# Second layer's output projection regrouped, its final quarter computed block by block with the norm's rows in PSUM; the first layer's conv taps and weight splits divided anew between the engines

## The chip, the cores and the metric

One core of one Trainium2 chip. The metric is the device time of one execution in microseconds (us): 1711.2 us, the median of 3 runs (1710.54 to 1713.39). Engines are called as in the profile: PE (matrix multiply), PEld (its weight loads), DVE (vector), ACT (scalar activation), POOL (general), SP (issues the DMAs).

## What is computed

A decoder block of two layers on 1024 tokens of 1024 channels, in float32.

```
layer 1:  a, g, z = split(x @ w_in + b_in)
          u = a * sigmoid(g);  u = causal depthwise conv(u), 31 taps, + b_dw
          u = silu(layer_norm_over_channels(u)) * silu(z)
          x1 = layer_norm(ALPHA * x + u @ w_out + b_out)
K, V    = x1 @ kv_w                       (three groups of 16 heads of 64)
layer 2:  q, z = split(x1 @ w_in)
          per head: 3 dilated windows of attention, merged by their softmax denominators -> o
          out = layer_norm(ALPHA * x1 + (o * silu(z)) @ w_out + b_out)
```

## The kernel before

Every product is made of three passes of a rounded type: each operand is split into a high part (a rounded copy) and a low part (the rest), and PE computes high x high, low x high and high x low into one PSUM bank. A weight of 128x1024 (512 KB) is loaded by SP (`wraw`), copied to `whi` (line 234 on ACT, 236 on POOL) and subtracted to `wlo` (line 243, on DVE if its running number is in `DVE_LO`, otherwise on POOL). `whi`, `wlo` and `wraw` have two buffers each.

**The order of the instructions** is made by a list scheduler (class `Order`): each step has an engine, a cost in us, a priority, the steps that it follows and the buffers that it takes and frees; a simulation with these costs picks, for each engine, the ready step with the lowest priority. The result is the order of each engine's queue; the costs are nowhere else in the program.

**Layer 1.** PE makes the projections `pa`, `pg` (8 channel blocks) and `pz`, in two halves of 512 tokens. The conv of each channel block and half has 31 taps: tap 0 is an ACT activation (line 400), taps 1 to n-1 are products on ACT (`cvt`, line 410) added on POOL (line 414), and taps n to 30 are fused multiply-adds on DVE (line 426) into a PSUM bank. n is `N_POOL`, 12 for the second halves of channels 4 to 7 and 10 for the other 12 convs. For those 12 ("merged") the two sums run side by side and one DVE add joins them (line 438); for the four others DVE starts from POOL's sum. The statistics of the channel norm follow (lines 451 to 505), then norm, silu and gate (lines 517 to 527), the split into `uh` and `ul` (532, 537), the output projection `po` (line 638) and the post-norm, whose result is transposed (`pt`, line 730) for layer 2.

**Layer 2** works by pairs of heads, eight of them; the matmuls of the next pair's projections (`pk`, `pq`, `pzb`, `pv`) lie between the small matmuls of the pair before. `finish` closes a pair: ACT widens the reciprocal denominators (`rx`), PE spreads them over the head's rows (`rb`, line 1302: four 128x128 products with the identity for each token half), DVE scales (line 1307), POOL multiplies by the gate (`on`, line 1312), ACT and DVE split. The joins of the two heads run on POOL (`op`, line 1275). Pairs 0 to 6 go through DRAM (`o_d`), the last pair directly into `uhb`/`ulb`.

**The out-projection of layer 2** has four quarters: token half h (outs[0], outs[1]) by column half ch. A quarter is 16 steps of 6 matmuls: four weights kp (channel blocks 2kp and 2kp+1) by four token blocks j, each j with its own PSUM bank. kp = 3 needs the last pair. Before, the last pair's attention was filled with kp 0 to 2 of quarters (0,0) and (0,1); then came kp 3 of (0,1) and (0,0), and then the two quarters of outs[1] whole, the last with its last two weights j by j. `evac` adds a bank to the residual `r` on DVE (lines 654 and 656; `r` was loaded from `x_d` and given the bias on POOL, line 610) and takes its statistics (line 663). `norm` then makes mean and 1/sd (672 to 683), centers on ACT (695), multiplies by the gain row (699) and adds the bias row (703), on DVE or POOL as `PATHS` says, and stores (707).

Of the kernel before, what the change touches and what calls it, by code (L numbers as in the profile page):

```python
# [28 lines left out]
N_POOL = dict.fromkeys(("d4", "d5", "d6", "d7"), 12)  # L29
# [4 lines left out]
DVE_LO = {0, 2, 3, 8, 9, 11, 12, 14, 15, 17, 19, 20, 23, 24, 25, 26, 27, 31, 33, 34, 35, 38, 39, 41, 42, 44, 45, 46, 90, 92, 93, 94, 98, 100, 101, 102, 103, 104, 105, 106, 108, 110, 111, 112, 113, 114, 115, 117, 118, 119, 124, 125, 126, 130, 131, 133, 134, 136}  # L34
PATHS = {(0, 1): 'dp', (1, 1): 'dd', (2, 1): 'pd', (3, 1): 'pd', (0, 0): 'pd', (2, 0): 'pd', (3, 0): 'dd'}
# [3 lines left out]
RELEASE = 0.25  # L39
ENGINES = ("pe", "act", "dve", "pool", "dma", "none")  # L40
# [9 lines left out]
class Step:  # L50
    def __init__(self, eng, cost, fn, prio, table, take):
        self.eng, self.cost, self.fn, self.prio, self.table, self.take = eng, cost, fn, prio, table, take
        self.waits, self.then, self.users, self.frees = 0, [], 0, []


class Order:
# [5 lines left out]
    def add(self, eng, cost, fn, prio, after=(), take=None, frees=(), table=None):  # L62
        step = Step(eng, cost, fn, prio, table, take)
# [12 lines left out]
    def run(self):  # L76
# [8 lines left out]
        while True:  # L85
# [28 lines left out]
            while events and events[0][0] <= now:  # L114
                _, _, _, other, step = heapq.heappop(events)
                for o in step.frees if other is None else ():
                    o.users -= 1
                    if not o.users:
                        live[o.take] -= 1
                for o in step.then:  # L120
                    if o.eng == other:
                        o.waits -= 1
                        if not o.waits:
                            heapq.heappush(heaps[other], (o.key, o))
# [6 lines left out]
def block_kernel(ctx: ExitStack, tc: tile.TileContext, x, xT, a_w_in, a_vec, a_w_out, rows,  # L131
# [74 lines left out]
    class Weight:  # L206


        def __init__(self, src, shape, pieces=1, hi_eng="act", spare=False):
# [4 lines left out]
            self.steps, self.spare = [], spare  # L214
# [3 lines left out]
        def piece(self, n, src, shape, i, pieces, hi_eng, hi_cost, lo_eng, lo_cost):  # L218
# [3 lines left out]
            @on("dma", 1.46 / pieces, (1, n) if pieces == 1 else (1, 0.5, 2 * i + 0.5, n), take=None if i else "raw")  # L222
            def fetch():
                if i == 0:
                    self.raw = wpool.tile([P] + shape, F32, name="wraw", tag="raw")
# [3 lines left out]
            @on(hi_eng, hi_cost, (0.5, n), [fetch], take=None if i else "b4" if self.spare else "whi")  # L229
# [8 lines left out]
            @on(lo_eng, lo_cost, (0.5, n), [hi], take=None if i else "b4" if self.spare else "wlo", frees=[self.first] if last else [])  # L238
# [7 lines left out]
        def part(self, name, shape):  # L246
            if self.spare:
                return b4(name, F32R).rearrange("p (k n) -> p k n", n=shape[1])
# [6 lines left out]
        def slots(self):  # L255
            return self.steps[0]
# [14 lines left out]
    def project(name, w, src, h, prio):  # L271
# [3 lines left out]
        def part(k):  # L275
            @on("pe", 0.68, prio + (k,), ([b.last] if k else []) + w.ready(k, KT) + src.steps[h][k],
# [166 lines left out]
    def mean_of(h, y, last):  # L443
# [3 lines left out]
        @on("pe", 0.86, (0, 0), [last, cst_in] + ([b.last] if b.first else h * [var[0].first]), take=None if b.first else "av")  # L447
# [62 lines left out]
    def apply(c, h, idx):  # L510
# [23 lines left out]
        @on("dve", 0.86, (0.5, c), [hi], take="hp", frees=[y.first])  # L534
# [49 lines left out]
    class Out:  # L584


        def __init__(self, h, row, src, prio, by_class=False):
# [4 lines left out]
            self.lazy = src is UA and h == 0  # L592
# [21 lines left out]
        def product(self, ch, kps, weight_of, banks, jk=False, end=False):  # L614
# [3 lines left out]
            if jk:  # L618
                cut = len(kps) - 2
                todo = todo[:4 * cut] + [(kp, j) for j in range(4) for kp in kps[cut:]]  # L620
            n = step_no("unit")
            for i, (kp, j) in enumerate(todo):
                self.part(ch, kp, j, ws[kp], banks[j], kp == kps[0], kp == kps[-1], n, i, end)

        def part(self, ch, kp, j, w, b, start, stop, n, i, end):
# [3 lines left out]
            @on("pe", 1.38, self.prio + (n, i), w.ready() + [s for k in ks for s in src[k, h].steps] +  # L629
                ([] if start else [b.last]), take=b.tag if start else None,  # L630
# [35 lines left out]
        def norm(self, j, dst_d, turned=None, paths={}):  # L666
# [18 lines left out]
            for ch in range(2):  # L685
                self.finish(j, ch, shift, dst_d, turned, paths.get((j, ch), "dp"))
# [226 lines left out]
    def scores23(a, g, o, gate):  # L913
# [24 lines left out]
        for i in range(2):  # L938
            bias = bias_of(a, g, i)
            part(i, 0.5, 0.83, [(slice(r * P, (r + 1) * P), slice(2 * r * P, (2 * r + 1) * P),  # L940
# [8 lines left out]
    def swap(made, prio):  # L949
# [4 lines left out]
        @on("pe", 0.25, prio, [made], take="cv")  # L954
# [90 lines left out]
    def vals(srcs, by_block, gate, n, end=False):  # L1045
# [26 lines left out]
        def part(t, kh, i):  # L1072
# [17 lines left out]
            @on("pe", 1.45, n + (i,), ws[kh].ready() + ready + ([b.last] if b.last else []),  # L1090
# [56 lines left out]
    def turn(a, blocks, after, frees):  # L1147
# [4 lines left out]
        @on("pe", 0.085 * n, (2.8, a.p, 4), after + a.flip, take="cv", frees=frees)  # L1152
# [136 lines left out]
    def finish(a, n):  # L1289
# [8 lines left out]
        @on("pe", 0.88, (2.8, a.p, 5), [widen] + a.turned[1], take="cv", frees=[widen])  # L1298
# [46 lines left out]
    for p in range(PAIRS):  # L1345
# [3 lines left out]
        a.sz, a.sz_step, a.op, a.op_slot, a.finished, a.stored = {}, {}, {}, {}, [], []  # L1349
# [31 lines left out]
    for h in range(2):  # L1381
        def fetch_u(h=h):
# [12 lines left out]
            for k in range(KT):  # L1395
                UB[k, h] = Box()
                UB[k, h].steps, UB[k, h].slots = list(got), []
# [12 lines left out]
    def weight_out(ch, kp, spare=False):  # L1410
# [102 lines left out]
```

## Time and profile before

| | |
|---|---|
| median of 3 runs | 1711.2 us |
| the profiled execution | 1710.37 us |
| its span, first to last instruction | 1708.6 us |
| PE / DVE / ACT / POOL busy, share of the span | 96% / 63% / 52% / 49% |
| mean granted clock of PE | 0.983 |
| layer 1 / layer 2 up to the last scores / last pair and out-projection | to about 436 us / to about 1563 us / to the end |

The page gives shares over the whole span, and the stages have different limits, so it is read by stretches. A line of the timeline has the start, the duration in us, the engine, the source line, the operation with its output and inputs, the number of instructions merged into the line, and in brackets the idle time before and what ended it. Durations of instructions in a row overlap, since each includes its latency: how often one can start is read from the starts.

### The profile page before, as it was taken

What the parts mean: (1) busy time and instruction counts of PE and PEld (TensorE: products, weight loads), DVE (VectorE), ACT (ScalarE), POOL (GpSimd) and SP (SyncE); (2) the same over time, 40 slices, a digit from 0 to 9 for tenths busy, and PEclk for the clock granted to TensorE, in tenths of its full rate; (3) what the DMA queues carried; (4) which work ended last, traced back from release to release, by engine and by line L of the source; (5) the groups of instructions that cost most, each with busy time, mean ns of one, the idle gap of its engine ahead of it and who ended that gap; (6) DMA issues with size and microseconds to landing.
All of it is one profiled execution on the core that took longest, in us unless ns stands there. A gap on an engine that the chain in (4) does not pass through costs nothing.

```text
span 1708.6 us, 25230 instructions
## 1 busy us (share of the span) xinstructions
PE 1637.9 (96%) x9396; PEld 1419.1 (83%) x9396; DVE 1074.4 (63%) x2293; ACT 887.9 (52%) x1986; POOL 834.1 (49%) x490
## 2 busy tenths in 40 slices
PE   8999968999899999999999999999999999999966
PEld 6888856767789988988988998898898899889855
DVE  7999999978664554554365365546536554653475
ACT  7666636265228525725743663664284275339432
POOL 5999957348333444444344435432432242233563
PEclk9999989999899999999999999999999999999988
DMA  5111111544211111101101101210120111135532
GB/s 190 50 50 41 59 37 50 174 140 155 74 38 38 38 38 62 37 29 65 45 26 48 64 26 38 66 47 25 38 75 26 38 62 38 38 103 186 193 99 86
DMA packets 43803, 116.67 MB, mean 68 GB/s; under 512 B 4512, under 2 KB 5792, under 8 KB 43680
## 3 DMA queue, kind: packets, MB, share of 16 engines
q1 hardware_dynamic: 43680, 115.06, 20.1%
q8 instruction: 74, 1.21, 0.3%
q14 instruction: 49, 0.40, 0.1%
HBM read 97.21 MB, written 17.83 MB: 67 GB/s over the span
## 4 chain that ended last, share of the span: by engine, by line
PE 69%; DVE 2%; ACT 1%; POOL 1%; DMA 1%; issue 0%; DVEq 0%; SPq 0%; POOLq 0%; ACTq 0%
PE pq L282 15%; PE pk L282 15%; PE pv L1099 15%; PE po L638 5%; PE pzb L282 5%; PE ptp L1156 4%; PE ps L866 3%; PE ps L867 3%; PE av L1175 2%; PE av L1172 2%; PE rb L1302 1%; DMA ulb<-o_d 1%; DVE x1b L1066 1%; POOL r L610 0%; DVE r L699 0%
## 5 line engine op out<-in xcount | busy, mean ns | idle before, releaser
L236 POOL TENSOR_SCALAR whi<-wraw 128x1024 fp32r<-128x1024 f32 x80 | 223.4, 2792 | 509.5 <-PE pv L1099 149.3
L243 POOL TENSOR_TENSOR wlo<-wraw,whi 128x1024 fp32r<-128x1024 f32 (+1 forms) x82 | 191.2, 2332 | 114.0 <-ACT whi L234 109.9
L414 POOL TENSOR_TENSOR y<-y,cvt 128x512 f32<-128x512 f32 x152 | 205.8, 1381 | 23.4 <-ACT cvt L410 18.6
L426 DVE SCALAR_TENSOR_TENSOR cva<-u,av,cva 128x512 f32<-128x512 f32 x308 | 209.0, 744 | 0.5
L822 DVE TENSOR_TENSOR kl<-pk,kd 64x512 fp32r<-64x512 f32 x192 | 132.2, 689 | 106.3 <-ACT kd L818 56.8
L1166 DVE TENSOR_TENSOR pl<-ptp,ph 128x384 fp32r<-128x384 f32 (+1 forms) x192 | 108.5, 587 | 105.1 <-ACT ph L1161 98.8
L870 DVE CUSTOM_DVE_ANT_0 s<-ps,bias 128x256 f32<-128x256 f32 (+1 forms) x384 | 122.6, 371 | 53.6 <-PE ps L867 53.3
L282 PE MATMUL pk<-x1h,whi 128*128 128x512 f32 x384 | 154.0, 401 | 0.0
L282 PE MATMUL pq<-x1h,whi 128*128 128x512 f32 x384 | 153.8, 401 | 0.0
L282 PE MATMUL pk<-x1h,wlo 128*128 128x512 f32 x384 | 150.6, 392 | 1.6 <-DVE wlo L243 1.6
L282 PE MATMUL pq<-x1h,wlo 128*128 128x512 f32 x384 | 150.7, 392 | 0.0
L282 PE MATMUL pq<-x1l,whi 128*128 128x512 f32 x384 | 150.5, 392 | 0.0
L282 PE MATMUL pk<-x1l,whi 128*128 128x512 f32 x384 | 150.2, 391 | 0.0
L852 ACT ACTIVATE qs<-pq 64x512 fp32r<-64x512 f32 x96 | 56.9, 593 | 174.3 <-PE pq L282 173.6
L1099 PE MATMUL pv<-whi,x1h 128*128 128x256 f32 x512 | 147.1, 287 | 0.0
L1099 PE MATMUL pv<-wlo,x1h 128*128 128x256 f32 x512 | 144.9, 283 | 0.0
L1099 PE MATMUL pv<-whi,x1l 128*128 128x256 f32 x512 | 144.9, 283 | 0.0
L410 ACT ACTIVATE cvt<-u,av 128x512 f32<-128x512 f32 x152 | 106.2, 719 | 53.9 <-POOL y L414 52.2
L818 ACT ACTIVATE kd<-pk 64x512 fp32r<-64x512 f32 x96 | 56.8, 592 | 141.7 <-PE pk L282 140.8
L1161 ACT ACTIVATE ph<-ptp 128x384 fp32r<-128x384 f32 (+1 forms) x192 | 93.0, 513 | 61.7 <-PE ptp L1156 47.2
L243 DVE TENSOR_TENSOR wlo<-wraw,whi 128x1024 fp32r<-128x1024 f32 (+1 forms) x60 | 98.9, 1649 | 32.2 <-POOL whi L236 16.9
L857 DVE TENSOR_TENSOR qs<-pq,qs 64x512 fp32r<-64x512 f32 x96 | 66.1, 688 | 77.4 <-ACT qs L852 75.1
(163 smaller groups left out, 4532.5 us busy)
## 6 DMA issues: line engine op xcount, KB each, us to landing
wraw<-in_w_k_dram SPq DMA_DIRECT2D x24, 512.0 KB, 3.4
wraw<-in_w_q_dram SPq DMA_DIRECT2D x24, 512.0 KB, 3.5
wraw<-in_w_v_dram SPq DMA_DIRECT2D x24, 512.0 KB, 3.5
wraw<-in_a_w_in_dram SPq DMA_DIRECT2D x22, 512.0 KB, 3.5
wraw<-in_a_w_out_dram SPq DMA_DIRECT2D x16, 512.0 KB, 3.5
wraw<-in_b_w_out_dram SPq DMA_DIRECT2D x16, 512.0 KB, 3.6
xraw<-in_xT_dram SPq DMA_DIRECT2D x16, 256.0 KB, 4.6
wraw<-in_w_z_dram SPq DMA_DIRECT2D x8, 512.0 KB, 3.4
```

What stands on the lines that cost most here:

```text
L236: nc.gpsimd.tensor_scalar(self.hi[:, s], self.raw[:, s], 1.0, None, op0=OP.mult)
L243: eng.tensor_sub(self.lo[:, s], self.raw[:, s], f32(self.hi[:, s]))
L282: nc.tensor.matmul(b.t, lhsT=u[:, k, :], rhs=v[h][:, k, :], start=k == 0 and i == 0, stop=k == KT - 1 and i == 2)
L410: nc.scalar.activation(q.t, src, AF.Copy, scale=wc)
L414: nc.gpsimd.tensor_add(y.t, y.t, q.t)
L426: nc.vector.scalar_tensor_tensor(y.t if s == TAPS - 1 and not merged else o.t, src, wc, y.t if s == n_pool else o.t, op0=OP.mult, op1=OP.add)
L638: nc.tensor.matmul(b.t, lhsT=u, rhs=v[:, k % 2, :], start=start and k == ks[0] and m == 0, stop=stop and k == ks[1] and m == 2)
L822: nc.vector.tensor_sub(d, src, f32(views(g, h, b, own, o.kd[i], own)[0]))
L870: nc.vector.tensor_tensor_reduce(s, ps, bias, op0=OP.add, op1=OP.max, scale=1.0, scalar=NEG, accum_out=acc)
L1099: nc.tensor.matmul(o, lhsT=cols((X1.hi, X1.lo)[u], u, kk), rhs=w[:, kk, :], start=k == 0 and m == 0 and t % 2 == 0, stop=k == KT - 1 and m ...
L1161: nc.scalar.activation(o.ph[:, :n * P], o.t[:, :n * P], AF.Copy)
L1166: nc.vector.tensor_sub(o.pl[:, :n * P], o.t[:, :n * P], f32(o.ph[:, :n * P]))
```

## The change

Six things are edited. (1) Layer 1's conv: `N_POOL` is 10 instead of 12 and the default 9 instead of 10, so 20 taps move from ACT and POOL to DVE. (2) `DVE_LO`: none of layer 1's weights (numbers 0 to 39) is split on DVE any more; of the out-projection's 16 (numbers 120 to 135) 11 are, instead of 7. The numbers between stay as they are. (3) `rb` is four transposes for each token half instead of four products. (4) The out-projection's order: kp 0 to 2 of quarter (1,0) follow those of (0,0) and (0,1), on the attention's banks, once the spreads are done; then kp 3 of (0,1), (0,0), (1,0); the last quarter (1,1) runs j by j with all four weights, whose halves lie in the two `xt` buffers that the first half's `uhb`/`ulb` leave, and the seven last weights are loaded into the `hw` buffers. The residual tiles of outs[1] are fetched earlier, and outs[0]'s statistics and norm get a late priority. (5) The gain and bias rows for outs[1] are copied to PSUM by ACT, and its norm is two fused DVE instructions per tile, `(r - mean) * gain` and `r * (1/sd) + bias`. (6) Several costs of the scheduler change, which can reorder queues anywhere; `MEAN_LATE` is 0 and changes nothing.

```diff
-N_POOL = dict.fromkeys(("d4", "d5", "d6", "d7"), 12)
+N_POOL = dict.fromkeys(("d4", "d5", "d6", "d7"), 10)
...
-DVE_LO = {0, 2, 3, 8, 9, 11, 12, 14, 15, 17, 19, 20, 23, 24, 25, 26, 27, 31, 33, 34, 35, 38, 39, 41, 42, 44, 45, 46, 90, 92, 93, 94, 98, 100, 101, 102, 103, 104, 105, 106, 108, 110, 111, 112, 113, 114, 115, 117, 118, 119, 124, 125, 126, 130, 131, 133, 134, 136}
-PATHS = {(0, 1): 'dp', (1, 1): 'dd', (2, 1): 'pd', (3, 1): 'pd', (0, 0): 'pd', (2, 0): 'pd', (3, 0): 'dd'}
+DVE_LO = {41, 42, 44, 45, 46, 90, 92, 93, 94, 98, 100, 101, 102, 103, 104, 105, 106, 108, 110, 111, 112, 113, 114, 115, 117, 118, 119} | set(range(124, 138)) - {132}
...
-                conv(n, int(what == "d"), N_POOL.get(group[i:i + 2], 10), group[i:i + 2] in MERGED, idx)
+                conv(n, int(what == "d"), N_POOL.get(group[i:i + 2], 9), group[i:i + 2] in MERGED, idx)
...
-            self.lazy = src is UA and h == 0
+            self.lazy = h == 0
...
             if jk:
-                cut = len(kps) - 2
-                todo = todo[:4 * cut] + [(kp, j) for j in range(4) for kp in kps[cut:]]
+                todo = [(kp, j) for j in range(4) for kp in kps]
...
+        def rows_to_psum(self, after):
...
+                @on("act", 0.6, (0.4, 1), after + [self.row.step[n, ch]], take=tag)
+                def move():
+                    b.t = bank("rowp", tag)
+                    nc.scalar.activation(b.t, self.row.t[n, ch], AF.Copy)
...
+        def norm_near(self, j, dst_d):
...
+                @on("dve", 0.68, (0, 4, j, ch), [aggr, g.step])
+                def gain():
+                    nc.vector.scalar_tensor_tensor(self.r[j, ch], self.r[j, ch], s.mv[:, 0:1], g.t,
+                                                   op0=OP.subtract, op1=OP.mult)
+
+                @on("dve", 0.68, (0, 4, j, ch), [gain, inverse, b.step])
+                def bias():
+                    nc.vector.scalar_tensor_tensor(self.r[j, ch], self.r[j, ch], s.sd, b.t, op0=OP.mult, op1=OP.add)
...
-                nc.tensor.matmul(q.t[:, j * P:(j + 1) * P], lhsT=q.x[:, j].rearrange("p i d -> p (i d)"), rhs=ident,
-                                 start=True, stop=True)
+                nc.tensor.transpose(q.t[:, j * P:(j + 1) * P], q.x[:, j].rearrange("p i d -> p (i d)"), ident)
+
+        a.spread.append(spread)
...
-    def weight_out(ch, kp, spare=False):
-        return Weight(b_w_out[ch, kp], [2, 512], spare=spare)
+    def weight_out(ch, kp, home=None):
+        return Weight(b_w_out[ch, kp], [2, 512], home=home, raw="hw" if kp == 3 or home else "raw",
+                      after=a.turned[1] if kp == 3 or home else ())
...
-    b00, b01 = banks(["pj"] * 4), banks(["pj"] * 4)
+    for ch in range(2):
+        for j in range(4):
+            outs[1].fetch(x1_d, j, ch, lambda: hp("r"), a.done23[0], "hp")
+    b00, b01, b10 = banks(["pj"] * 4), banks(["pj"] * 4), banks(["av", "av", "cv", "cv"])
     outs[0].product(0, range(3), weight_out, b00)
     outs[0].take_in(0, b00, False)
-    outs[0].product(1, range(4), weight_out, b01)
+    outs[0].product(1, range(3), weight_out, b01, close=False)
+    outs[1].product(0, range(3), weight_out, b10, close=False, gate=a.spread)
+    outs[0].product(1, [3], weight_out, b01, begin=False)
     outs[0].take_in(1, b01)
-    b00 = banks(["av", "av", "cv", "cv"])
-    outs[0].product(0, [3], weight_out, b00)
+    b00 = banks(["pj"] * 4)
+    outs[0].product(0, [3], weight_out, b00, end=True)
     outs[0].take_in(0, b00)
+    outs[1].product(0, [3], weight_out, b10, begin=False)
+    outs[1].take_in(0, b10)
     for j in range(4):
-        outs[0].norm(j, out)
-    for ch in range(2):
-        for j in range(4):
-            outs[1].fetch(x1_d, j, ch, lambda: hp("r"), a.turned[1], "hp")
-    for ch in range(2):
-        bs = banks(["pj"] * 4)
-        outs[1].product(ch, range(4), lambda ch, kp: weight_out(ch, kp, ch == 1 and kp == 3), bs, jk=ch == 1)
-        outs[1].take_in(ch, bs)
+        outs[0].norm(j, out, path="pp" if j > 1 else "dp")
+    outs[1].rows_to_psum([b.last for b in b10])
+    homes = [Home([b.last for b in b00]) for _ in range(2)]
+    bs = banks(["pj"] * 4)
+    outs[1].product(1, range(4), lambda ch, kp: weight_out(ch, kp, homes[kp // 2]), bs, jk=True)
+    outs[1].take_in(1, bs)
     for j in range(4):
-        outs[1].norm(j, out, paths=PATHS)
+        outs[1].norm_near(j, out)
```

## Rows read from the trace of the kernel before

**Rows 1.** The page, busy time of each engine over the whole span.
```profile
PE 1637.9 (96%) x9396; PEld 1419.1 (83%) x9396; DVE 1074.4 (63%) x2293; ACT 887.9 (52%) x1986; POOL 834.1 (49%) x490
```

**Rows 2.** Windows, whole kernel: stretch, its us; PE, PEld, DVE, ACT, POOL busy; clock; DMA.
```profile
40.00:212.80 172.80, 172.80 (x750) 140.49 (x749) 170.63 (x251) 113.85 (x161) 168.05 (x121) 1.00 0.15 48
212.80:232.00 19.20, 9.69 (x43) 7.70 (x41) 19.20 (x3) 10.65 (x17) 18.09 (x15) 0.81 0.03 13
232.00:338.10 106.10, 96.24 (x375) 73.64 (x376) 102.68 (x135) 43.27 (x61) 55.80 (x35) 0.94 0.29 99
338.10:436.40 98.30, 88.27 (x375) 66.95 (x374) 81.74 (x122) 55.05 (x84) 61.78 (x37) 0.95 0.45 149
436.40:1562.56 1126.16, 1118.10 (x7094) 1002.59 (x7094) 589.68 (x1609) 579.56 (x1504) 442.19 (x222) 1.00 0.14 47
1611.00:1695.30 84.30, 70.45 (x298) 56.81 (x296) 49.55 (x72) 24.38 (x34) 44.68 (x27) 0.92 0.26 87
```

**Rows 3.** Timeline of POOL, DVE and PE in layer 1.
```profile
204.71 26.17 POOL L414 TENSOR_TENSOR y<-y,cvt 128x512 f32<-128x512 f32 x21
...
212.87 19.10 DVE L243 TENSOR_TENSOR wlo<-wraw,whi 128x1024 fp32r<-128x1024 f32 x1
...
232.02 0.80 PE L282 MATMUL pz<-xh,wlo 128*128 128x512 f32 x1 [9.53 <-DVE wlo L243]
...
336.78 1.39 DVE L426 SCALAR_TENSOR_TENSOR y<-u,av,cva 128x512 f32<-128x512 f32 x2
```

**Rows 4.** The chain that ended last, from 1600 us: start, us, engine, tile, line.
```profile
1600.57 0.65 PE ptp L1156 x6
1601.22 2.75 PE po L638 x12
...
1610.91 1.78 PE rb L1302 x16
...
1616.40 6.84 POOL r L610 x5
...
1631.64 22.46 PE po L638 x92
...
1658.14 2.21 DVE wlo L243
...
1660.40 34.83 PE po L638 x142
...
1704.14 1.20 DVE r L703 x2
```

**Rows 5.** Windows of one source line: L243 (DVE, POOL), L426 (DVE), L414 (POOL).
```profile
25.00:338.10 313.10, 43.07 (x16) 28.89 (x12) 0.97 0.19 64
...
25.00:338.10 313.10, 211.78 (x314) 0.97 0.19 64
...
0.00:231.00 231.00, 182.59 (x137) 0.99 0.22 72
```

**Rows 6.** L243 on DVE, 20 to 440 us: duration in ns, min/median/max.
```profile
L243 DVE TENSOR_TENSOR wlo<-wraw,whi x23: 1207/1429/19098, 29.5 to 435.0; 128x1024 fp32r<-128x1024 f32 x23
```

**Rows 7.** Groups of instructions, POOL 22 to 300 us, DVE 25 to 338 us.
```profile
L414 POOL TENSOR_TENSOR y<-y,cvt 128x512 f32<-128x512 f32 x152 | 205.8, 1381 | 23.4 <-ACT cvt L410 18.6
L243 POOL TENSOR_TENSOR wlo<-wraw,whi 128x1024 fp32r<-128x1024 f32 x10 | 24.1, 2407 | 11.7 <-ACT whi L234 11.7
...
L537 DVE TENSOR_TENSOR ul<-y,uh 128x512 fp32r<-128x512 f32 x8 | 11.6, 1492 | 0.0
```

**Rows 8.** Windows of L638 alone, PE: layer 2's projection matmuls before 1611 us.
```profile
1570.00:1611.00 41.00, 26.29 (x102) 18.34 (x102) 1.00 0.75 264
```

**Rows 9.** Tile r on DVE, 1560 us to the end: duration in ns, min/median/max.
```profile
L656 DVE SCALAR_TENSOR_TENSOR r<-r,po x16: 674/687/691, 1594.4 to 1695.3; 128x512 f32<-128x512 f32 x16
L663 DVE BATCH_NORM_STATS2 st<-r x16: 683/694/695, 1633.6 to 1696.5; 128x6 f32<-128x512 f32 x16
...
L699 DVE TENSOR_TENSOR r<-r,row x12: 679/1747/1870, 1645.3 to 1700.1; 128x512 f32<-128x512 f32 x12
```

More of the change, by code (lines that the diff above doesn't have):

```diff
@@ L39 @@
 RELEASE = 0.25
+MEAN_LATE = 0.0
 ENGINES = ("pe", "act", "dve", "pool", "dma", "none")
@@ L60, in __init__, with add @@
         self.bufs, self.steps = bufs, []
-    def add(self, eng, cost, fn, prio, after=(), take=None, frees=(), table=None):
-        step = Step(eng, cost, fn, prio, table, take)
+    def add(self, eng, cost, fn, prio, after=(), take=None, frees=(), table=None, late=0.0):
+        step = Step(eng, cost, fn, prio, table, take, late)
         for o in after:
@@ L115, in run @@
                 _, _, _, other, step = heapq.heappop(events)
+                if other == "late":
+                    heapq.heappush(heaps[step.eng], (step.key, step))
+                    continue
                 for o in step.frees if other is None else ():
@@ L122, in run @@
                         o.waits -= 1
-                        if not o.waits:
+                        if not o.waits and o.late:
+                            heapq.heappush(events, (now + o.late, len(order), -2, "late", o))
+                        elif not o.waits:
                             heapq.heappush(heaps[other], (o.key, o))
@@ L255, in slots, with __init__, part @@
         def slots(self):
-            return self.steps[0]
+            return [self.home.slot] if self.home else self.steps[0]
+    class Home:
+        def __init__(self, after):
+            self.slot, self.t, self.n = slot("xt", after), None, 0
+        def part(self):
+            self.t = self.t if self.t is not None else xtile("whome")
+            self.n += 2
+            return self.t[:, self.n - 2:self.n, :]
     class Bank:
@@ L445, in mean_of @@
         summed[h].append(y)
-        @on("pe", 0.86, (0, 0), [last, cst_in] + ([b.last] if b.first else h * [var[0].first]), take=None if b.first else "av")
+        @on("pe", 0.86, (0, 0), [last, cst_in] + ([b.last] if b.first else h * [var[0].first]), take=None if b.first else "av", late=MEAN_LATE)
         def mm(start=b.first is None, stop=len(summed[h]) == KT):
@@ L532, in hi @@
             nc.scalar.activation(g.hi, y.t, AF.Copy)
-        @on("dve", 0.86, (0.5, c), [hi], take="hp", frees=[y.first])
+        @on("dve", 1.3, (0.5, c), [hi], take="hp", frees=[y.first])
         def lo():
@@ L612, in fetch, with product @@
             self.held[j, ch] = [get] if take else after
-        def product(self, ch, kps, weight_of, banks, jk=False, end=False):
+        def product(self, ch, kps, weight_of, banks, jk=False, end=False, begin=True, close=True, gate=[]):
             ws = {kp: weight_of(ch, kp) for kp in kps}
@@ L618, in product, with part @@
             if jk:
-                cut = len(kps) - 2
-                todo = todo[:4 * cut] + [(kp, j) for j in range(4) for kp in kps[cut:]]
+                todo = [(kp, j) for j in range(4) for kp in kps]
             n = step_no("unit")
             for i, (kp, j) in enumerate(todo):
-                self.part(ch, kp, j, ws[kp], banks[j], kp == kps[0], kp == kps[-1], n, i, end)
-        def part(self, ch, kp, j, w, b, start, stop, n, i, end):
+                self.part(ch, kp, j, ws[kp], banks[j], begin and kp == kps[0], close and kp == kps[-1], n, i, end, gate)
+        def part(self, ch, kp, j, w, b, start, stop, n, i, end, gate):
             src, h = self.src, self.h
             ks = (2 * kp, 2 * kp + 1)
-            @on("pe", 1.38, self.prio + (n, i), w.ready() + [s for k in ks for s in src[k, h].steps] +
-                ([] if start else [b.last]), take=b.tag if start else None,
+            @on("pe", 1.4, self.prio + (n, i), w.ready() + [s for k in ks for s in src[k, h].steps] +
+                (list(gate) if start else [b.last]), take=b.tag if start else None,
                 frees=w.slots + ([s for k in ks for s in src[k, h].slots] if end else []))
@@ L952, in swap @@
         o = Box()
-        @on("pe", 0.25, prio, [made], take="cv")
+        @on("pe", 0.15, prio, [made], take="cv")
         def fold_in():
```

66 lines of the change are left out of this document (47 added, 19 removed).

## The prediction

> **What bounds the kernel now.** I read the page first, then windows by stage, then timelines where a stage is not PE's. PE is busy 96% of the span [rows 1], but that is a mean over three different stages. In the windows the reader is to see this [rows 2]: from 436 to 1563 us PE is busy 1118.1 of 1126.2 us, and nothing but less PE work shortens that. From 40 to 338 us DVE is the full engine: 170.6 of 172.8, 19.2 of 19.2, 102.7 of 106.1 us. PE, which keeps up until 213 us, then idles 9.5, 9.9 and 10.0 us in the three stretches up to 436 us, at a mean clock of 0.81 to 0.95, so part of the time at the 1.2 GHz level. After 1611 us PE is again not full: 70.5 of 84.3 us, at 0.92.
>
> The timeline shows one odd instruction in DVE's stage [rows 3]: a weight's low half on DVE takes 19.10 us, where the median is 1.43 [rows 6]. It begins inside a run of 21 POOL adds that goes from 204.71 to 230.88 us without a gap (1.25 us each), and ends one us after the run. PE then waits 9.53 us for it. So DVE, reading two SBUF operands, got no turn until POOL paused. The conv's last tap on DVE ends at 338.2 us, and the rest of layer 1 hangs on it.
>
> At the end the chain [rows 4] leaves PE twice: POOL's residual adds hold up the join of the last pair until 1631.6 us, and DVE's gains hold up a low half until 1660.4 us. The last matmul ends at 1695.2 us, and 13.4 us of norm and stores follow.
>
> **The change, part by part.** The sum is made against the profiled execution, 1710.4 us with a span of 1708.6; the median is 0.8 us above it.
>
> *Layer 1.* Removed from DVE between 25 and 338 us: 16 low halves, 43.07 us [rows 5], the 19.10 among them. Added: 20 taps (12 convs by one, 4 by two) at 211.78/314 = 0.674 us [rows 5], 13.5 us. Net on DVE 13.5 - 43.1 = -29.6 us. Is DVE still last? POOL gets 16 x 2.41 = 38.6 us and loses 20 x 1.38 = 27.6 [rows 7], net +11.0. By 231 us it had done 137 of its 152 taps [rows 5, 7]; some ten low halves more by then (24 us, or 18 taps) leave it at 119 of 132, and 13 taps are 18 us: it stays well ahead of a DVE that ends at 338 - 30 = 308. ACT loses 20 products and was never full [rows 2]. PE can follow: its idle time of 29.4 us is there to be given back. What I take off: the eight `ul` of the first half cost 1.49 us each [rows 7], and an uncontended one is one DVE pass, as the 0.68 of a residual gain [rows 9]; POOL will be busier then, so I count half of that excess of 6.5 us once more. -29.6 + 3.3 gives **-26 us**. Six more low halves go to POOL between 338 and 410 us; it has 61.8 busy of 98.3 there [rows 2], so I count them at nothing. What covers them is PE's work on the previous weight; without that cover they cost at most 6 x 2.4 = 14 us. Nor do I count the eight quarter pieces at the start, where POOL waits. Bounds: -33 (all PE idle and the slow clock gone) to -5 (a new long wait of some 18 us, and some of the 14).
>
> *The spread.* 16 matmuls take 1.78 us; six transposes of the same size take 0.65 [rows 4], so eight take 0.87. It saves 0.91 us in each of eight pairs; seven lie where PE is full, **-6.4 us**, the eighth in the end stage. If they ran at the old interval, eight of them would still be half as many, so nothing below 0.
>
> *New costs in the scheduler* reorder queues between 436 and 1563 us. PE idles 8 us there [rows 2]: at best -6, at worst some low halves later; I take 0 with ends of -5 and +5.
>
> *The end.* The projection has 4 x 16 x 6 = 384 matmuls, 102 of them before 1611 us [rows 8], 282 after. At 2.75/12 = 0.229 us [rows 4] these are 64.6 us, while PE has 84 us from rb to its last matmul: some 18 us are waits and the slow clock behind them. After the change PE has, behind the spread, 42 matmuls of the first two quarters and 72 of quarter (1,0), 26 us, before it needs the last pair, where it had 10. The join's lateness (9 us) fits into that. Then 1611 + 0.9 + 64.6 = 1676.5 us for the last matmul. Behind it the last block's two DVE passes (add, statistics, 0.69 each [rows 9]), the small ones (0.4) and four fused passes, which I price like line 656, also one SBUF and one PSUM operand, 0.69 [rows 9]: 4.5 us; then the store, which now takes from DVE's last instruction at 1705.3 us [rows 4] to 1708.6, 3.3 us. So PE allows 1684.3, -24 us.
>
> DVE allows less. Its work from the first closing step (1612 + 26 + 1.4 = 1639 us): 12 tiles of add and statistics, 16.6 us; five low halves at 1.2 to 2.2 [rows 4, 6], 6 to 11; four gains at 0.68 to 1.87 [rows 9], 3 to 7.5; small ones of the first half, 2; four final blocks at 4.5, 18. Together 46 to 55 us, so an end between 1688 and 1697. These are durations, which overlap by some 7%, which takes 3 to 4 us off. I take 1688.5, near the lower end because POOL's additions are spread, **-20 us** (this holds the eighth spread). Ends: -25 and -5. The queue behind moved steps: SP issues eight loads of r earlier and the seven late weights after the last attend, in the `hw` buffers, none later than before; POOL has eight adds earlier, in time it spent waiting; ACT gets four copies and loses eight centerings.
>
> Sum: -26 - 6.4 - 20 = -52.4 us, so 1658.0 for the execution, 1659 for the median.
>
> **A rule against the row.** Row: the 19.10 us above is a wait for a whole run of POOL's instructions [rows 3]. The Trainium skill says (SBUF — State Buffer, Who interferes with whom) that a DVE instruction with two SBUF inputs and a GpSimd instruction that reads SBUF lock each other out, and that the second is blocked until the first finishes. By that rule the low half would have taken at most 1.2 + 1.4 = 2.6 us, an estimate from rows; the trace agrees that they collide and not on how long. By that rule the third rival below could not cost more than some 5 us.
>
> **Rivals.** (A) Layer 1's gain is caught by the next wait. The gate stage has 12 DVE instructions with two SBUF operands, and POOL now runs taps without a pause just there. One more wait of 19.1 - 1.4 = 17.7 us leaves -8 of the 26: 1677. For it: the `ul` already take 1.49. Against: POOL's run is over by about 280 us.
>
> (B) The end becomes DVE's, or PE waits anyway. Half of quarter (1,0)'s banks are those of the spread, free only after DVE's scale, which waits for POOL's join; and the last quarter's four weights can be split only once quarter (0,0) is done, 5.5 us before PE needs the first, on the DVE queue that also carries adds and statistics. Then only 5 us remain: 1674. For it: the DVE sum above. Against: in the first 8 us there are six steps on free banks. (A) and (B) together give 1692.
>
> (C) Slower than before: the long wait multiplies. DVE holds all late low halves (11 of 16) while POOL runs residual adds and outs[0]'s norm, 12 instructions that can follow each other without a gap. A wait of 17.7 us there also stalls PE, which then runs at the lower level for a while (the mean clock of the end stage is 0.92 [rows 2]); with 2 us for that, an estimate, it is some 20 us for each. From the third on they outweigh 52 us: 1711 + 8 = 1719. For it: the 19.10. Against: the median of the 23 low halves is 1.43 us [rows 6].
>
> (D) The parts do what they say, but a reordered queue loses it all: no change.
>
> **The numbers.** Forecast 0.58 (1644 to 1668: the two lower ends, -33 and -25 with -6.4, reach 1647, less 3 for reordering), A 0.16, B 0.14, both 0.05, C 0.04, D 0.03. The range goes from 1644 to 1688, which takes in A, B and their spread and leaves out the rest. What a measurement can tell from no change is about 0.2%, 3.4 us: faster 0.58 + 0.16 + 0.14 + 0.05 = 0.93, same 0.03, slower 0.04.
>
> **What would show it.** Layer 1: no low half on DVE before the first layer is over, the last conv tap at about 308 us instead of 338, the first `pq` of layer 2 some 26 us earlier, and PE's idle time before that below 10 us. Spread: 64 instead of 128 instructions at line 1302's place, 0.9 us for each pair. End: no PE wait over 2 us behind the spread, last matmul to the end below 12 us. Wrong would be: DVE instructions of over 5 us in the gate stage or among the last low halves (A, C); a PE wait for `uhb`, for a bank or for a low half behind 1611 us (B); a stretch between 436 and 1563 us that is not 6 us shorter.

## The result and the profile after

The changed kernel takes 1668.4 us (median of 4 runs, 1668.0 to 1668.4) against 1712.3 us (4 runs, 1710.5 to 1714.1) of the kernel before beside it: ratio 0.974, 95% interval 0.973 to 0.976. I had forecast 1659, range 1644 to 1688. The direction is right and the time within the range, but the gain is 43.9 us instead of 52.4, and its parts are not the ones I had summed. The profiled execution took 1668.02 us, its span is 1666.2.

One thing must be known to read every number below. The kernel before has two groups of times. Of its 44 executions beside the experiments, 22 took 1692.5 to 1698.0 us (median 1694.3) and 22 took 1709.6 to 1713.6 (median 1711.5), with nothing between; the executions shown so far all fell into the upper group. Against the lower one the changed kernel gains 26 us, not 43.

The windows of the kernel after, with the columns of [rows 2], cut at the same events (last conv tap, first `pq`, last uploads, last spread, last matmul):

```profile
40.00:212.80 172.80, 172.57 (x749) 140.10 (x748) 171.27 (x261) 103.97 (x147) 162.93 (x116) 1.00 0.15 48
212.80:232.00 19.20, 19.20 (x76) 14.09 (x75) 16.06 (x21) 10.11 (x15) 18.06 (x12) 1.00 0.19 62
232.00:309.40 77.40, 75.83 (x320) 59.63 (x319) 75.05 (x105) 39.97 (x56) 56.73 (x38) 1.00 0.36 118
309.40:415.90 106.50, 96.10 (x400) 72.81 (x398) 79.49 (x117) 55.16 (x82) 79.06 (x46) 0.94 0.41 139
415.90:1541.50 1125.60, 1114.29 (x7048) 996.57 (x7047) 594.64 (x1612) 579.64 (x1507) 444.19 (x223) 1.00 0.15 47
1591.00:1655.80 64.80, 64.76 (x290) 53.41 (x288) 44.77 (x77) 23.54 (x34) 21.44 (x16) 1.00 0.26 93
```

The reader is to see four things. Ahead of the last tap PE's idle time is gone: 19.4 us in two stretches [rows 2], now 1.6, and the clock there is 1.00. Behind the tap the stretch grew from 98.3 to 106.5 us: PE is busy 7.8 us more and idle for 10.4 us as it was for 10.0. The pairs take 1125.6 us, as before (1126.2). At the end PE is full: the stretch is 19.5 us shorter, of which 13.8 were idle time of PE, 0.9 the spread, and 4.8 is what is left, in a stretch whose clock was 0.92 and is 1.00.

In the timeline of DVE after, the last tap, which answers to the last of [rows 3]; it ends at 309.4 us instead of 338.2:

```profile
308.04 1.39 DVE L443 SCALAR_TENSOR_TENSOR y<-u,av,cva 128x512 f32<-128x512 f32 x2
```

The view of tile `pq`, before and after (count, duration in ns, first and last start): layer 2 starts 20.1 us earlier. Other profiles of the same two kernels, taken with the experiments, have it at 438.3 and 440.5 us before and at 417.8 after, so a difference of 2 us in this place says little.

```profile
L282 PE MATMUL pq<-x1h,whi x384: 387/389/777, 436.0 to 1520.8; 128*128 128x512 f32 x192
```

```profile
L299 PE MATMUL pq<-x1h,whi x384: 389/389/774, 415.9 to 1499.7; 128*128 128x512 f32 x192
```

The view of tile `rb`, before and after: half as many instructions, the first 19.8 us and the last 20.8 us earlier; as the last group itself is 0.9 us shorter, the stretch from the first spread to the last is as long as it was.

```profile
L1302 PE MATMUL rb<-cs,rx x128: 272/275/276, 595.1 to 1612.4; 128*128 128x128 f32 x128
```

```profile
L1370 PE MATMUL rb<-cs,rx x64: 270/272/274, 575.3 to 1591.6; 128*128 128x128 f32 x64
```

The chain that ended last, after; it answers to [rows 4]. It leaves PE only behind the last matmul:

```profile
1590.95 0.87 PE rb L1370 x8
1591.82 63.95 PE po L654 x282
1655.80 0.69 DVE r L672
...
1659.79 1.32 DVE r L721 x2
1661.10 0.66 DVE r L726
1661.76 0.66 DVEq L1584
```

PE's waits in the pairs, 416 to 1591 us, after (engine, line, what it waited for: us, times, longest). Before, the first row was 0.5 us, once, and the last two were not there:

```profile
PE av L1243 <- DVE pl L1234: 3.0, 3, 1.1
...
PE po L654 <- DMA ulb<-o_d: 1.1, 1, 1.1
PE ps L934 <- DVE op L1376: 0.7, 2, 0.4
```

So the span's 42.4 us come from: up to the first `pq` -20.1; from there to the last spread about 0; last spread to last matmul 84.3 to 64.8, -19.5; behind it 13.4 to 10.4, -3.0. The open questions were what in layer 1 gave the 20 us, where the spreads' 6.4 us went, and which part of the end did it.

### The profile page after: what moved, and what is told of

It is laid out like the page before. It is cut to its first block, busy times and chain, and to the rows that moved or that the text cites. A ratio compares the mean times of both kernels' runs of the same rounds, so it can differ in the third digit from the quotient of the medians.

```text
span 1666.2 us, 25048 instructions
## 1 busy us (share of the span) xinstructions
PE 1623.9 (97%) x9332; PEld 1406.4 (84%) x9332; DVE 1039.7 (62%) x2289; ACT 868.3 (52%) x1962; POOL 838.5 (50%) x490
## 4 chain that ended last, share of the span: by engine, by line
PE 70%; DVE 3%; ACT 2%; DMA 1%; issue 1%; POOL 0%; DVEq 0%; SPq 0%; POOLq 0%
PE pk L299 15%; PE pv L1167 15%; PE pq L299 15%; PE po L654 6%; PE pzb L299 5%; PE ptp L1224 4%; PE ps L934 3%; PE ps L935 3%; PE av L1243 2%; PE av L1240 2%; DMA ulb<-o_d 1%; DVE x1b L1134 1%; DVE kl L890 1%; DVE r L767 0%; PE rb L1370 0%
## 5 line engine op out<-in xcount | busy, mean ns | idle before, releaser
L249 POOL TENSOR_TENSOR wlo<-wraw,whi 128x1024 fp32r<-128x1024 f32 (+1 forms) x103 | 237.5, 2308 | 88.4 <-ACT whi L240 84.2
L443 DVE SCALAR_TENSOR_TENSOR cva<-u,av,cva 128x512 f32<-128x512 f32 x328 | 222.4, 747 | 0.9
L431 POOL TENSOR_TENSOR y<-y,cvt 128x512 f32<-128x512 f32 x132 | 170.1, 1311 | 12.7 <-ACT cvt L427 9.4
L1083 ACT ACTIVATE s<-s,nm 128x128 f32<-128x128 f32 (+1 forms) x256 | 113.7, 464 | 0.0
L427 ACT ACTIVATE cvt<-u,av 128x512 f32<-128x512 f32 x132 | 90.9, 717 | 43.2 <-POOL y L431 42.5
```

Source lines behind the costliest of these rows:

```text
L249: eng.tensor_sub(self.lo[:, s], self.raw[:, s], f32(self.hi[:, s]))
L431: nc.gpsimd.tensor_add(y.t, y.t, q.t)
L443: nc.vector.scalar_tensor_tensor(y.t if s == TAPS - 1 and not merged else o.t, src, wc, y.t if s == n_pool else o.t, op0=OP.mult, op1=OP.add)
L1083: nc.scalar.activation(s, s, AF.Exp, scale=SCALE, bias=a.nm2[:, 2 * i + n, r:r + 1], accum_out=a.d23[:, g - 1, i, n, r:r + 1])
```

## The experiments

All stages in us, from the tile views, the chains and DVE's timelines. "Pairs" is from the first to the last spread, "end" from the last spread to the end of the last matmul, "tail" from there to the end of the span.

| kernel | last tap | first pq | pairs | end | tail | median |
|---|---|---|---|---|---|---|
| before (upper group) | 338.2 | 436.0 | 1015.8 | 84.3 | 13.4 | 1711.5 |
| before, again (b1, one execution) | 342.9 | 440.5 | 1015.5 | 84.5 | 13.4 | 1715.1 |
| before, again (b2, one execution) | 340.5 | 438.3 | 1015.7 | 84.3 | 13.4 | 1712.6 |
| after | 309.4 | 415.9 | 1015.7 | 64.8 | 10.4 | 1668.4 |
| after, again (f2) | 310.9 | 417.8 | 1015.3 | 64.8 | 10.5 | 1668.6 |
| before, low half 19 on POOL (e1) | 323.6 | 425.6 | 1015.7 | 84.1 | 13.4 | 1700.9 |
| before, layer 1 changed (e2) | 313.2 | 425.0 | 1015.6 | 85.7 | 13.3 | 1700.1 |
| after, old order costs (e3) | 313.1 | 424.1 | 1011.1 | 65.0 | 10.6 | 1673.0 |
| after, spread as products (e4) | 310.7 | 417.2 | 1019.9 | 65.8 | 10.5 | 1673.7 |
| after, layer 2's old costs (e5) | 309.4 | 415.9 | 1009.4 | 70.3 | 10.5 | 1668.1 |
| after, ul's old cost (e6) | 313.5 | 429.3 | 1015.4 | 64.8 | 10.5 | 1677.0 |
| after, norm as before (e7) | 311.0 | 417.4 | 1015.8 | 64.8 | 19.1 | 1677.6 |
| after, old costs but ul's (f1) | 314.6 | 422.6 | 1011.5 | 64.9 | 10.7 | 1671.7 |
| after, six low halves on DVE (f4) | 311.4 | 420.0 | 1015.2 | 64.8 | 10.5 | 1670.6 |

**The long wait alone (e1).** One low half of the kernel before moves to POOL.

```diff
-DVE_LO = {0, 2, 3, 8, 9, 11, 12, 14, 15, 17, 19, 20, 23, 24, ...
+DVE_LO = {0, 2, 3, 8, 9, 11, 12, 14, 15, 17, 20, 23, 24, ...
```

> The kernel before with one edit: weight 19 (the fourth of pz), whose low half took 19.10 us on DVE, is split on POOL. Theory (one starved wait): no DVE instruction of over 5 us is left in layer 1, the last conv tap ends at 318 to 321 us instead of 338.2, PE's wait of 9.53 us goes, the first pq of layer 2 starts 12 to 18 us earlier, total 1694 to 1700 us. Rival (DVE is full of work anyway, the wait only shifts): the tap ends 1.4 us earlier and the total falls by less than 3 us, above 1709. Second rival (POOL is as late with it, behind the same run of adds): PE waits about as long, for POOL, total 1704 to 1712.

Median 1700.9 us (1699.6 to 1703.5), tap 14.6 us and first `pq` 10.4 us earlier. Neither rival holds, and the theory's numbers were too good, because the next low half met the next run of adds. Timelines of POOL and DVE of this kernel:

```profile
216.54 14.94 POOL L414 TENSOR_TENSOR y<-y,cvt 128x512 f32<-128x512 f32 x12
...
224.59 7.97 DVE L243 TENSOR_TENSOR wlo<-wraw,whi 128x1024 fp32r<-128x1024 f32 x1
```

The run ends at 231.48, the low half at 232.56, as the 19.10 us one ended 1.1 us behind its run [rows 3]. So the wait is not a property of low half 19: another one was caught, in a shorter run.

**Layer 1's edits alone (e2).**

```diff
-N_POOL = dict.fromkeys(("d4", "d5", "d6", "d7"), 12)
+N_POOL = dict.fromkeys(("d4", "d5", "d6", "d7"), 10)
-DVE_LO = {0, 2, 3, 8, ..., 38, 39, 41, 42, ...
+DVE_LO = {41, 42, ...
-                conv(n, int(what == "d"), N_POOL.get(group[i:i + 2], 10), ...
+                conv(n, int(what == "d"), N_POOL.get(group[i:i + 2], 9), ...
```

> The kernel before with the change's layer 1 alone: the two counts of taps and no low half of weights 0 to 39 on DVE; order costs, spread, end as before. Theory (layer 1 gives what the two traces show, 20.1 us, and nothing later takes it back): 1692 us, 1690 to 1694; first pq at about 416 us. Rival (part of the 20 us came from the new order costs, or the reordered queues take part of it back): 1696 to 1702. By my forecast's step for layer 1 alone it would be 1686.

Median 1700.1 us (1697.1 to 1701.9): the rival. The tap comes 25.0 us earlier, as forecast, but the first `pq` only 11.0. Where the 14 us between went is seen in the stretch behind the tap. PE's waits there (313 to 425 us):

```profile
PE pt L730 <- POOL r L703: 4.8, 5, 1.6
PE po L638 <- ACT whi L234: 4.7, 1, 4.7
PE pt L730 <- DVE x1l L746: 3.6, 2, 2.4
PE po L638 <- POOL wlo L243: 1.3, 1, 1.3
```

In the window 313.2 to 425.0 us PE is busy 97.3 us and idle 14.5, against 88.3 and 10.0 in [rows 2]: 9.0 us of work that it had not got ahead with (306 matmuls `po` of the out-projection behind the tap instead of 270), and 4.5 us of waits. The taps and the low halves were changed together here; no run takes the taps alone. Note also that 1700 us is 6 us above the lower group of the kernel before: alone, these edits make the time steady, they do not beat the kernel's better executions.

**The order costs (e3).** All eight costs of the list scheduler as before; the instructions are those of the changed kernel.

```diff
-            @on("pe", 0.69, prio + (k,), ...
+            @on("pe", 0.68, prio + (k,), ...
-        @on("dve", 1.3, (0.5, c), [hi], take="hp", frees=[y.first])
+        @on("dve", 0.86, (0.5, c), [hi], take="hp", frees=[y.first])
...
-        @on("pe", 0.44, (2.8, a.p, 5), [widen] + a.turned[1], take="cv", frees=[widen])
+        @on("pe", 0.88, (2.8, a.p, 5), [widen] + a.turned[1], take="cv", frees=[widen])
```

> The changed kernel with all eight order costs of before (spread 0.88 among them); same instructions, other order. Theory (the new order took back the spread's 6.4 us between the first pq and the last spread): the waits of PE for pl (3.0 us) and for ulb (1.1 us) go, this stretch is 4 to 6 us shorter, total 1662 to 1664.5 us. Rival (the shorter spread itself uncovers those waits, whatever the order): the stretch stays within 1 us, total 1667 to 1670. A shift in layer 1 or in the end is told apart by the first pq (416.2 us) and by the stretch behind the last spread (75.2 us).

Median 1673.0 us (1671.0 to 1675.4), so the total misses the theory; the stages show why. The pairs are 4.6 us shorter, as expected, and PE's wait for `pl` is back at 0.5 us, once:

```profile
PE po L654 <- DMA ulb<-o_d: 0.6, 1, 0.6
PE av L1243 <- DVE pl L1234: 0.5, 1, 0.5
PE ps L934 <- DVE op L1376: 0.4, 1, 0.4
```

But not all of the 4.6 us is time won: nine matmuls of `pq` more (some 2 us) lie ahead of the first spread here, 987 between the spreads instead of 996. From the first `pq` to the last matmul, with the same work between but for four transposes, it is 1236.0 us against 1239.9, and 1238.2 in the second profile of the changed kernel (f2). And the first `pq` is at 424.1 us, where e2 has it. So the new costs do two opposite things: they give 6 to 8 us in layer 1 and take 2 to 4 behind it.

**The spread (e4).**

```diff
-                nc.tensor.transpose(q.t[:, j * P:(j + 1) * P], q.x[:, j]..., ident)
+                nc.tensor.matmul(q.t[:, j * P:(j + 1) * P], lhsT=q.x[:, j]..., rhs=ident,
+                                 start=True, stop=True)
```

> The changed kernel with the spread as four products with the identity again, its order cost left at 0.44, so that every queue keeps its order. Theory (PE is the bound there and the transposes do save): 0.9 us more for each of eight pairs, total 1674 to 1676 us. Rival (the saving falls into waits of PE that end no earlier): less than 3 us more, under 1671.5.

Median 1673.7 us (1671.9 to 1674.4), 5.2 us more than the changed kernel: more than the rival allows, less than the theory's 7 us. Within one order the transposes save 4.2 us in the pairs and 1.0 at the end. The windows between the first and the last spread, of this kernel and of the changed one, show where the rest is:

```profile
576.51:1596.21 1019.70, 1014.28 (x6437) 908.09 (x6435) 527.34 (x1430) 530.25 (x1376) 413.72 (x214) 1.00 0.18 59
575.26:1590.79 1015.53, 1008.27 (x6381) 901.13 (x6380) 526.87 (x1430) 529.76 (x1376) 413.57 (x214) 1.00 0.18 59
```

PE is busy 6.0 us less with the transposes, near the 6.4 of the forecast, but idle 1.8 us more: the waits for `ulb` (1.1) and `op` (0.7) of the changed kernel are not among this kernel's, while its waits for `pl` are the same 3.0 us. So the theory holds for most of the saving, and the rival for 1.8 us.

**Layer 2's costs alone (e5).** Five of e3's eight costs: 0.5, 0.25, 1.45, 0.085, 0.88.

> The changed kernel with five of the eight order costs of before, those of layer 2's own steps (0.5, 0.25, 1.45, 0.085 and 0.88 for the spread); projections, ul and out-projection keep the new ones. Theory (two separate effects of the order: the new costs give 8 us in layer 1 and take 4.6 us in the pairs): first pq at 415 to 417 us, 1011 us from the first to the last spread, total 1663 to 1664.5 us. Rival (the pairs' order hangs on the state in which layer 2 starts, or on the projections' 0.69): 1014 to 1016 us between the spreads, total 1667 to 1669.5.

The first `pq` and the pairs do what the theory said, yet the median is 1668.1 us (1665.8 to 1670.1). The chain of this kernel shows the other side:

```profile
1583.32 0.87 PE rb L1370 x8
1584.19 69.39 PE po L654 x306
```

There are 306 matmuls behind the last spread instead of 282: 24 of them, 5.5 us, were moved out of the pairs into the end. From the first `pq` to the last matmul it is 1237.7 us against 1239.9, which the medians do not tell apart (f2 has 1238.2). Times between two events compare two orders only if the same work lies between them.

**The cost of ul, out and in (e6, f1).** e6 sets only the 1.3 back to 0.86; f1 keeps only the 1.3 and sets the other seven back.

> The changed kernel with one order cost of before: 0.86 instead of 1.3 for the low halves ul of layer 1. Theory (this one cost makes the better order of layer 1): first pq at 423 to 425 us, total 1675 to 1678 us. Rival (the costs of the projections' matmuls, 0.69 and 1.4, make it): first pq at 415 to 418 us, total 1667 to 1670 us.

> The changed kernel with seven of the eight order costs of before; only the 1.3 for ul stays new. Theory (the ul cost makes layer 1's order, the others only cost time in the pairs): first pq at 415 to 418 us as in the changed kernel, first pq to last matmul 1235 to 1237 us as with all old costs (1239.9 in the changed kernel), total 1663.5 to 1666 us. Rival (the good order of layer 1 needs the new costs together, as a single better draw of the scheduler): first pq at 421 to 430 us, total 1670 to 1678 us.

e6: first `pq` 429.3, median 1677.0 us (1673.9 to 1679.0): without it layer 1's order is 13 us worse. f1: first `pq` 422.6, median 1671.7 us (1671.4 to 1673.9): the rival. With the others old it brings only 1.5 us (424.1 to 422.6); PE then waits 5.5 us for a residual add of DVE. So the 1.3 is needed and not enough. But it does not take all of the new costs: e5 keeps only three of them, the 1.3, 0.69 and 1.4, and has its first `pq` at 415.9 like the changed kernel. Which of the other two is needed beside it, or whether both are, was not run.

**The last norm (e7).** outs[1] gets the norm of before with its table of engines, and no rows in PSUM.

```diff
-    outs[1].rows_to_psum([b.last for b in b10])
...
-        outs[1].norm_near(j, out)
+        outs[1].norm(j, out, path=PATHS)
```

> The changed kernel with outs[1]'s norm as before: ACT centres, gain and bias rows from SBUF on DVE or POOL by the table of before; no rows in PSUM. The order of the last quarter's matmuls stays. Theory (the fused norm with rows in PSUM shortens what follows the last matmul): last matmul to end 12.5 to 15 us instead of 10.4, total 1670.5 to 1674 us. Rival (the tail is short since the last quarter runs block by block; the rows in PSUM matter little): 10 to 11.5 us, total under 1669.5 us.

Median 1677.6 us (1676.7 to 1678.9): 9 us more, all in the tail, and more than the theory's 2 to 5. The chain of this kernel behind the last matmul goes through POOL, which does its gains (line 768) and biases (772):

```profile
1661.19 4.83 POOL r L768 x3
1666.02 3.34 POOL r L772 x2
1669.36 1.22 POOL r L768
```

In the regrouped end the new norm is thus worth some 9 us. This run takes away the fused form, the choice of engine and the rows in PSUM together, and its table of engines was made for the old order, whose tail was 13.4 us; which of these carries the 9 us is not shown. That the other 13 of the end's 22 us go with the regrouping and the spread is a subtraction: no run takes the regrouping, or the eleven low halves on DVE, alone.

**The six late low halves (f4).** The changed kernel with 31, 33, 34, 35, 38, 39 in `DVE_LO` again.

> The changed kernel with the low halves of six late weights of layer 1 (31, 33, 34, 35, 38, 39) back on DVE. Theory (PE's own work bounds what follows the conv; the six cost only the waits for POOL's low halves that the trace shows, 3.0 us, and a slow clock after them): first pq at 411 to 415 us, total 1663.5 to 1667.5 us. Rival (POOL's queue with these six is what holds layer 1's end, the up to 14 us that the prediction left out): first pq at 402 to 410 us, total under 1662 us. Third (the new order it makes is worse): first pq above 417 us.

First `pq` 420.0, median 1670.6 us (1670.1 to 1672.0): the third case. PE's wait for a POOL low half before `po` falls from 2.0 to 0.6 us, and the order it makes is slower all the same. PE now waits for POOL's post-norm, which it does not in the changed kernel:

```profile
PE pt L798 <- POOL r L771: 4.5, 5, 1.6
```

So moving the six gains nothing, but the run cannot tell their price from that of the order, and whether POOL's queue holds the end of layer 1 stays open.

**Again, for the two groups (b1, b2, f2).** The kernel before twice, the changed one once, all unedited.

> The kernel before, unchanged, for a second profile: its executions on the chip of the first four experiments fell into two groups, 1692 to 1698 us and 1709 to 1714 us, with nothing between. Theory (the 19.10 us wait of one low half decides the group): an execution of the lower group has no DVE instruction of over 5 us beside POOL's run of adds (or one shorter by over 10 us), its last conv tap ends 15 us or more earlier than 338.2, and the stretches behind the first pq of layer 2 last as long as before. Rival (the groups come from later, the end or the pairs): last tap and first pq stand where they were, and the 16 us are missing in a stretch behind them.

> The kernel before once more, for a profile of its lower group. If this execution takes 1692 to 1698 us: theory (the starved low half decides) expects that low half at under 8 us, the last conv tap below 326 us and the stretches from the first pq on as long as in the first profile; rival (a later cause): tap at 338 and the difference behind. If it takes 1709 to 1715 us: both expect the low half at 18 to 20 us once more.

> The changed kernel, unchanged, beside executions of the kernel before on this chip, where those fall into two groups (about 1694 and 1711 us). Theory (the changed kernel has no DVE instruction left that can be starved in layer 1, so it has one group): all executions within 1665 to 1671 us. Rival (the changed kernel has a second group too, not met in its first four executions): some executions 8 us or more above the others.

b1 took 1715.1 us and b2 1712.6: both upper group, so they decide nothing between theory and rival. They do repeat the wait (19.04 and 19.12 us). POOL and DVE of b2:

```profile
207.88 26.14 POOL L414 TENSOR_TENSOR y<-y,cvt 128x512 f32<-128x512 f32 x21
...
215.98 19.12 DVE L243 TENSOR_TENSOR wlo<-wraw,whi 128x1024 fp32r<-128x1024 f32 x1
```

f2: median 1668.6 us, five of six executions from 1667.7 to 1670.4 and one at 1674.5. That is one group, if with one stray; its ratio to all executions of before beside it is 0.979 (0.974 to 0.985).

No version beat the changed kernel: the nearest, e5, is level with it.

## Why the prediction was right in sign and 9 us off

**Layer 1, -26 forecast, -20.1 between the profiles.** The step on DVE was right: the tap moved by 28.7 us (forecast 29.6), 25.0 with the edits alone. The step that failed is "PE can follow: its idle time of 29.4 us is there to be given back". Only 19.4 of that lies ahead of the last tap. The 10.0 behind it are waits of the transposes `pt` for the post-norm's parts and of the out-projection for `ul` and `uh`; as much idle time stayed there (10.4), in part for other causes. PE's waits behind the tap, before:

```profile
PE pt L730 <- DVE x1l L746: 5.4, 3, 2.9
PE po L638 <- DVE ul L537: 2.0, 2, 1.7
PE po L638 <- ACT uh L532: 1.5, 1, 1.5
```

and after:

```profile
PE pt L798 <- DVE x1l L814: 6.5, 6, 2.3
PE po L654 <- POOL wlo L249: 2.0, 2, 1.8
PE pk L299 <- POOL wlo L249: 1.0, 1, 1.0
```

PE, no longer held up, was not ahead with the out-projection either, so 7.8 us of its work came to stand behind the tap (301 matmuls `po` instead of 270). What could be given back was the idle time ahead of the last dependence, 19.4 us, and what the slow clock had cost there. The term that I had left at nothing, the six low halves on POOL, comes to 3.0 us of PE's waits (the last two rows); whether they cost the total as much is open, since f4, with them back on DVE, has another order.

The second fault is in what I took for the cause. "New costs in the scheduler reorder queues between 436 and 1563 us" left layer 1 out. With the edits alone the first `pq` comes only 11.0 us earlier (e2); the other 7 to 9 (to 417.8 or 415.9) are the new order (e3, e6, f1), a thing that no row of the kernel before could have priced.

**The spread, -6.4 forecast, 0 between the profiles.** The duration was right (1.78 to 0.87 us for each pair, 64 instructions for 128), and so was the saving of PE's time: 6.0 us within one order (e4). What failed is that less PE work would shorten the stretch by as much. PE in the windows from the first `pq` to the last spread, before and after:

```profile
436.01:1610.75 1174.74, 1166.62 (x7425) 1046.43 (x7424) 610.16 (x1653) 608.56 (x1582) 459.29 (x232) 1.00 0.17 56
415.87:1590.79 1174.92, 1162.48 (x7377) 1040.05 (x7376) 615.73 (x1655) 608.39 (x1584) 471.38 (x241) 1.00 0.17 57
```

PE is busy 4.1 us less (eight of layer 1's transposes have come into the window) and idle 4.3 us more. Of these 4.3, the waits for `ulb` and `op`, 1.8 us, come with the shorter spread itself, since e4, with the products in the same order, does not have them; and 2.5 us, the waits for `pl` (3.0 instead of 0.5), come with the new order, since e4 has them too and e3 does not. This is the term that I set to 0 with ends of -5 and +5. My test in advance, "a stretch that is not 6 us shorter", came true.

**The end, -20 forecast, -22.4 measured.** The working for PE was right to 0.7 us: 65.5 us forecast from the last spread to the last matmul, 64.8 measured, with no wait; POOL had all 12 residual additions done when the last join came. The mis-sized term is DVE's allowance. From the first closing step to DVE's last instruction I took 46 us (1639 to 1685.2, the stores' 3.3 us before 1688.5). It was 42.0 (1619.7 to 1661.8), and DVE is as good as full there, 40.7 us of this window:

```profile
1619.00:1661.80 42.80, 36.76 (x163) 30.10 (x161) 40.68 (x77) 16.17 (x26) 18.35 (x13) 0.97 0.29 103
```

So DVE's sum was the right bound, with prices too high. Adds and statistics start 0.60 us apart, where I had 0.69 less some 7%, and four low halves came behind that step, at 1.2 us each, where I had five at up to 2.2. From the timeline of DVE:

```profile
1629.63 0.69 DVE L679 BATCH_NORM_STATS2 st<-r 128x6 f32<-128x512 f32 x1
1630.23 0.67 DVE L672 SCALAR_TENSOR_TENSOR r<-r,po 128x512 f32<-128x512 f32 x1
1630.82 0.69 DVE L679 BATCH_NORM_STATS2 st<-r 128x6 f32<-128x512 f32 x1
```

Behind the last matmul DVE took 6.0 us instead of my 4.5, because it still had steps of earlier blocks to do, and the stores 4.4 instead of 3.3.

**The sum.** 5.9 us missing in layer 1 and 6.6 in the pairs, 2.4 more at the end: 10 us short, which is the span's 42.4 for 52.4.

**The rivals.** A did not show: no DVE low half is left in layer 1, and no wait of 17 us came up elsewhere. B cost nothing: PE has no wait behind the spread, although DVE is as good as full. C had its conditions and did not come either: in the changed kernel two low halves on DVE begin inside a run of 12 POOL adds (timelines of POOL and DVE, from 1575 us), and each got its turn after one of them.

```profile
1575.68 17.01 POOL L627 TENSOR_TENSOR r<-r,row 128x512 f32<-128x512 f32 x12 [0.58 <-DMA r<-x_d]
```

```profile
1580.83 2.23 DVE L249 TENSOR_TENSOR wlo<-wraw,whi 128x1024 fp32r<-128x1024 f32 x1 [0.22 <-ACT whi L240]
1590.17 1.38 DVE L249 TENSOR_TENSOR wlo<-wraw,whi 128x1024 fp32r<-128x1024 f32 x1 [1.23 <-ACT whi L240]
```

That a reordered queue takes a gain back (D) held in part for the spread.

**The rule on locks.** These rows are the usual case, and the rule holds for it. The Trainium skill (SBUF — State Buffer, Summary: rules for kernel authors) has the second instruction blocked until the first finishes. By that a low half takes at most some 2.6 us, an estimate from rows. The trace agrees with that for most, not for all. In the 14 profiles here 77 low halves on DVE begin inside an add of POOL that another add follows at once; 73 of them take 2.4 us at most. The other four, 19.10, 19.04, 19.12 and 7.97 us, are all in the conv of kernels made from the one before, and end 1.1 us behind the last add of POOL's run. Three of the four are one and the same low half in the three profiles of the kernel before, so 4 in 77 is a count and not a rate. So the rule stands, with an exception that costs up to 18 us; I had read the exception as the way of things. What makes it is not settled: all four began 0.54 to 0.68 us into an add, but four others that began as far in (0.60 to 0.69 us) took 1.7 to 1.8 us.

**What stays open.** That the lower group of the kernel before is the one without this wait was argued and not shown: the excess of the wait, 19.1 - 1.4 = 17.7 us, fits the distance of the groups, 17.2, but no execution of the lower group was profiled. That e1 and e2, whose edits both touch layer 1's low halves, have one group each in ten executions (1699.6 to 1703.5 and 1697.1 to 1701.9) speaks for it, though both can have another order too. If it is so, layer 1 changed little against those executions (first `pq` at some 436 - 17 = 419 us, an estimate, against 416 to 418), and the 26 us of gain against them are nearly all the end's.

## What to carry to other kernels

An odd long instruction in one profile is a reason to look at the spread of the kernel's times first: a wait that hangs on how two queues happen to meet may be there in only some executions (argued here, not shown), and then taking it away is worth its full price only in those. Here only the idle time of PE that lay ahead of the last dependence that moved was given back; split idle time there before using it as a bound. Where a list scheduler writes the queues, an edit of a cost can redraw the order far from its own step (one cost moved the first `pq` by 13 us here), so an edit and the order that comes with it are to be timed apart, and a gain in one stretch is counted only when the same work lies in it.

## What was not expected of the hardware

A DVE instruction with two operands in SBUF that meets a run of POOL adds mostly waits for one add at most (2.23 us for a low half), but four times in 77 it got no turn until the run was over, 14 adds later in three of them and 5 in the fourth, while POOL went on at its full pace (26.14 us for 21 adds). One and the same program, in 44 executions, had two groups of times 17 us apart.
